# Forgetting-attention heads 0 to 3 projected as three seven-product chunks behind the z units, with two attention workers and the token sums on GpSimd

## The chip, the cores and the metric

The kernel runs on one core of one Trainium2 chip. The metric is the device time of one execution in microseconds (us); the number to beat is the median of three runs. Engine names are those of the profile: PE is TensorE (PEld its weight loads), DVE VectorE, ACT ScalarE, POOL GpSimd, SP SyncE. PE reads its operands from the on-chip memory and writes banks of 128x512 float32, which the other engines empty.

## The reference

One decoder block on 512 tokens of width 1024, all float32: a gated delta rule with 8 heads (called GDN) and a forgetting attention with 8 heads (called FOX) side by side, merged by two sigmoid gates, and a squared-ReLU MLP behind it.

```python
u = rmsnorm(x, norm_mix_g)
gq, gk, gv, gz, ga, gb, fq, fk, fv, ff, gate_a, gate_b = split(u @ w_in)
# A: causal conv(4)+SiLU on gq,gk,gv; L2 norm; exact chunked gated delta rule -> o_a
y_a = (rmsnorm(o_a, gdn_norm_g) * silu(gz)) @ w_proj_gdn
# B: per head RMSNorm of fq, fk; c = cumsum(log_sigmoid(ff + bias)); for each block of 128 queries
s = q @ k.T * d**-0.5 + c[queries, None] - c[None, keys]        # causal
o_b = softmax(s) @ v
y_b = o_b @ w_proj_fox
h = x + (sigmoid(gate_a) * y_a + sigmoid(gate_b) * y_b) @ w_out
out = h + relu(rmsnorm(h) @ w_up)**2 @ w_down
```

## The kernel before

**Number format.** Every large product is made in three passes: weights and activations are each split into a rounded part `hi` and a remainder `lo`, and PE adds hi·hi, hi·lo and lo·hi. The weights of `w_in` come in *units* of 128x1024 (512 KB). `seq` (L151 to L187) lists all units in the order in which they are used. `unit()` (L260) hands out the next one and, while it does, splits units two places ahead (`LA_SPLIT`) with an ACT copy (`hi`, L256) and a DVE subtraction (`lo`, L257), and loads units three places ahead (`LA_RAW`).

**Two ways of projecting.** `dense()` (L269) takes one unit and makes 24 matmuls of 128x512 (L275, L276, L279): the z units (`zgate`, L1071) and the GDN units (`project`, L592, which follows with a convolution of three DVE steps and a SiLU on ACT) go this way. `stream()` (L981) takes *chunks* of 512 output columns and computes each by seven products of quarter size instead of eight (Strassen's scheme in Winograd's form), named P1 to P7. One product is one unit and 24 matmuls of 128x256 (L1011). The weight quarters P1, P2, P3 are plain loads on the SP queue; those of P5, P6, P7, P4 are sums, and are made by an adding DMA on the POOL queue onto a quarter that is on the chip already (`load`, L219). The other operand, the sums of token quarters, is made once by `factors_u` (L426), which reads the normalised tokens back from DRAM (`ud`), subtracts on DVE (L448) and splits (L286, L287), into `uforms`. Each product is added into its quarter of the output by an ACT copy or a DVE addition (L991, L993). A chunk holds at most two of three PE banks at a time (`mmfree`).

**FOX heads 0 to 3 before** use neither: `fox_pair` (L950) makes two heads from six units, with 288 matmuls of 128x256 (L961, L962, L964) and no saved product. Heads 4 to 7 are the first three chunks of `stream`, and the gates four more.

**Work in the background.** The rest runs as generators in `tasks`. `tick()` (L127) advances each of them by one step; `dense`, `zgate`, `fox_pair` and `stream` call it after every few microseconds of projection. The tasks that matter here are:
- `head` (L612): four steps that turn a GDN head's q, k, v into the matrices of the chunked rule; the fourth waits until `decays` (L560) has made that head's decay matrices.
- `group_chain` (L831): once the four heads of a group are done, `invert` (L659) inverts the triangular matrices, with a loop of 31 pairs of DVE instructions (L681, L683) that gives way to the next tick whenever its counted cost passes `INV_STEP[g]`; then `scan` (L781) runs the recurrence over four chunks.
- `decays(1, ...)`: starts its work when group 0's chain is gone.
- `fox_worker` (L866): takes FOX heads from `fq`, one after the other, and runs softmax attention on them in about ten ticks. `hold[0]` keeps workers from taking a new head.
- `outputs_in` (L1111): waits until the stream's last chunk has begun and all chains and workers are done, then reads the GDN outputs back; `merge_gdn` in the stream's last places needs it.

**Order.** The Python order gives the priorities; a planner with its own estimate of durations then places every engine's instructions, so the small matmuls of the tasks lie among the large ones. The main line (L1086 to L1102) is: z units 0 to 4; GDN group 0 (12 units); `fox_pair(0)`; start of `factors_u`; `fox_pair(1)`; z units 5 to 7; GDN group 1 (12 units, with attention held); then the stream of 49 products (`STREAM`), the projections behind both branches, and the MLP, which the change does not touch.

Of the kernel before, what the change touches and what calls it, by code (L numbers as in the profile page):

```python
# [7 lines left out]
F32 = mybir.dt.float32  # L8
# [7 lines left out]
P = 128  # L16
# [23 lines left out]
LA_SPLIT = 2  # L40
INV_STEP = (2500, 900)


def hybrid_block(tc, a, out):
# [106 lines left out]
    seq = [("w_ab", 0)] + [("w_z", i) for i in range(NZ1)]  # L151
    seq += [("w_gdn", i) for i in range(12)] + [("w_fox", i) for i in range(12)]
    seq += [("w_z", i) for i in range(NZ1, H)] + [("w_gdn", 12 + i) for i in range(12)]

# [45 lines left out]
    def load(n):  # L200
        nme, i = seq[n]
        if nme in FACTOR:
            w, c, s_ = i
            q, old = FACTOR[nme]
            if old is None:
                if w == "w_st":
                    raw = (swp if nme == "P1" else wraw).tile([P, D], F32, tag="raw", name=nm("sraw"))
                else:
                    raw = fresh[2 if nme == "P2" else s_].tile([P, D], F32, tag="raw", name=nm("draw"))
                nc.sync.dma_start(raw, a[w][c, q, s_])  # L210
            elif (nme, i) in LONE:
                if n not in begun:
                    begin(n)
                raw = begun[n]
                nc.gpsimd.dma_start(raw, a[w][c, 2, s_], accum_op=ALU.add)
            else:
                raw = factors[old, i]
                assert seq.index((old, i)) < len(units)
                nc.gpsimd.dma_start(raw, a[w][c, q, s_], accum_op=ALU.add)  # L219
            factors[nme, i] = raw  # L220
            raws[n] = raw, [slice(0, D)]
            return
        w = 256 if nme == "w_ab" else D
        raw = wraw.tile([P, D], F32, tag="raw", name=nm("raw"))
        cuts = [slice(0, 512), slice(512, D)] if 0 < n < 3 else [slice(0, w)]
        for c in cuts:
            nc.sync.dma_start(raw[:, c], a[nme][i][:, c])
        raws[n] = raw, cuts
# [6 lines left out]
    def prefetch_new(n):  # L235

        for m in range(pos[0], min(len(seq), n)):
            if fresh and m not in raws and seq[m][0] in FACTOR and FACTOR[seq[m][0]][1] is None and seq[m][1][0] != "w_st":
                load(m)
            if seq[m] in LONE and m not in begun:  # L240
                begin(m)
# [39 lines left out]

    def split(src, scale=None, dst=None):

        hi, lo = dst or (page(F32R, "hi")[:, :], page(F32R, "lo")[:, :])
        if scale is None:
            act.copy(hi, src)  # L286
            vec.tensor_tensor(lo, src, hi.bitcast(F32), op=ALU.subtract)  # L287
        else:
# [137 lines left out]
    def factors_u():  # L426
        lo, hi = slice(0, 256), slice(256, 512)
        for part in range(2):
# [9 lines left out]
            for p in ("P5", "P7", "P6", "P3"):  # L438
                yield
                x = s1 if p == "P5" else s2  # L440
                for f in range(2):
# [5 lines left out]
                                    "P3": (c[k + 4][:, lo], s2[:, o], ALU.add)}[p]  # L447
                    vec.tensor_tensor(x[:, o], in0, in1, op=op)  # L448
                xh_, xl_ = split(x)
                for f in range(2):  # L450
# [387 lines left out]

    def gdn_group(g, box):
        AT = atp.tile([P, NI, P], F32, tag="AT", name=nm("AT"))  # L840
        hd = drp.tile([5, NCH, P, G, P], F32, tag=f"hd{g}", name=f"hd{g}")
        hts = []
        for i in range(G):
            h = g * G + i
            ys = []
            for j in range(3):
                ys.append(project(h, j))
                tick()
            hts.append(start(head(h, AT, *ys, box, hd)))
        return start(group_chain(g, AT, hd, hts))  # L850


    fq = []
    hold = [False]
    taken = [0]
# [10 lines left out]
    def fox_worker(after=None):  # L866
# [3 lines left out]
        while taken[0] < H:  # L870
            if taken[0] >= len(fq) or hold[0]:
                yield
                continue
# [75 lines left out]

    def fox_pair(hp):  # L950
        vts = ([], [])
        for pn in range(3):
            us = [unit("w_fox"), unit("w_fox")]
            pg2 = [page(s="fqk"), page(s="fqk")]
            for t2 in range(2):
                ps = mmps("fx")
                for tb in (2 * t2, 2 * t2 + 1):
                    o = ps[:, (tb % 2) * 256:(tb % 2 + 1) * 256]
                    for k in range(KT):
                        w = us[k // 4][0][:, (k % 4) * 256:(k % 4 + 1) * 256]  # L960
                        mm(o, uhi[k][:, cs(tb)], w, start=(k == 0), stop=False)  # L961
                        mm(o, ulo[k][:, cs(tb)], w, start=False, stop=False)  # L962
                    for k in range(KT):
                        mm(o, uhi[k][:, cs(tb)], us[k // 4][1][:, (k % 4) * 256:(k % 4 + 1) * 256], start=False,  # L964
                           stop=(k == KT - 1))
                    if tb % 2 == 0:
                        tick()
                if pn < 2:
                    act.copy(pg2[t2], ps)
                else:  # L970
                    for j in range(2):
                        (vec.tensor_copy if j else act.copy)(
                            v3(pg2[j][:, 2 * t2 * P:(2 * t2 + 2) * P], 2), v3(ps[:, :], 2)[:, :, cs(j)])
                tick()
            if pn < 2:
                fq.append((2 * hp + pn, pg2, vts[pn]))
            else:
                for v, x in zip(vts, pg2):
                    v += [x[:, cs(c)] for c in range(NCH)]

    def stream(parts, other):  # L981

# [11 lines left out]

        for p, c in STREAM:
            if p is None:
# [16 lines left out]
            done = parts[c][2]  # L1013
            at[0] = c
            if p == "P1":
# [73 lines left out]
    start(decays(0, box, gt))  # L1089
    fws = [start(fox_worker())]  # L1090
    ch0 = gdn_group(0, box)
    fox_pair(0)
    fu = start(factors_u())
    fox_pair(1)
    start(decays(1, box, ch0))
    hold[0] = True
    for h in range(NZ1, H):
        zgate(h)
    ch1 = gdn_group(1, box)
    hold[0] = False  # L1100
    finish(fu)
    fws += [start(fox_worker()) for _ in range(1, NFW)]  # L1102

# [37 lines left out]
    parts += [gate_chunk(i, to) for to in (sga, mg) for i in range(2)]  # L1141
    stream(parts, merge_gdn)

# [296 lines left out]
def _layout(inputs):  # L1440
# [20 lines left out]
    fx = w[:, 4112:7184].reshape(D, 3, H, P)  # L1461
    pan = []
    for hp in range(2):
        for h in (2 * hp, 2 * hp + 1):
            pan.append(np.concatenate([fx[:, 0, h], fx[:, 1, h]], axis=1))
        pan.append(np.concatenate([fx[:, 2, 2 * hp], fx[:, 2, 2 * hp + 1]], axis=1))
    o["w_fox"] = c(np.stack(pan).reshape(6, 2, 4, P, 256).transpose(0, 1, 3, 2, 4).reshape(12, P, D))
    q, k, v = [[fx[:, j, h] for h in range(H)] for j in range(3)]
# [3 lines left out]

    st = np.stack(st).reshape(7, 2, 4, P, 2, 256)
    o["w_st"] = c(np.stack([st[:, j, :, :, l] for j, l in ((0, 0), (0, 1), (1, 1), (1, 0))], 1)
                  .transpose(0, 1, 3, 2, 4).reshape(7, 4, 1, P, D))
    o["w_z"] = units(w[:, 3072:4096])
# [43 lines left out]
```

## Time and profile before

| what | value |
|---|---|
| runs of before | 981.11, 982.70, 982.94 us (median 982.7) |
| span of the profiled execution | 980.2 us, 2.5 us under the median; the page gives no other time for it |
| PE busy | 970.8 us, 99% |
| DVE, ACT, POOL busy | 710.9, 605.0, 240.2 us |
| granted TensorE clock | 1.000 |
| L961, L962, L964 (`fox_pair`) | first at 122.4 us, last at 213.2 us |
| L1011 (`stream`) | first at 324.7 us, last at 543.5 us |

A PE instruction is drawn from its start to its modelled end, and the next one starts before that end. A busy PE therefore says only that something was under way; what a matmul costs is read from the distance between starts, or from the chain of waits, which cuts overlapping instructions at the next start. A stage is judged by its own window, since the mean over the span mixes stages with different loads on DVE and ACT.

### The profile page before, as it was taken

The numbers are of one execution on the slowest core, as the hardware profiler recorded it, in microseconds if no ns is written. First come the engines' busy times: TensorE is split into PE (matmuls) and PEld (weight loads), VectorE is DVE, ScalarE is ACT, GpSimd is POOL, SyncE is SP. The second block draws the span as 40 slices with busy tenths as digits, with TensorE's granted clock in tenths as the row PEclk, the third lists the DMA queues.
The fourth block names the chain that finished last, engine by engine and source line by source line (L and its number), as shares of the span: only waits on it lengthen the run. The fifth ranks groups of instructions, "written<-read, shape, count | busy, mean of one in ns | idle before, by whom it ended". The sixth has DMA issues, their size and how long they took to land.

```text
span 980.2 us, 17198 instructions
## 1 busy us (share of the span) xinstructions
PE 970.8 (99%) x6545; PEld 874.8 (89%) x6545; DVE 710.9 (73%) x1204; ACT 605.0 (62%) x1050; POOL 240.2 (25%) x236
## 2 busy tenths in 40 slices
PE   8999999999999999999999999999999999999998
PEld 6788899998888999999999888889989989988986
DVE  6877778566577789855656535889896697698596
ACT  7766444766564787867656422678755765666761
POOL 1544120202533513522320005312121121121110
PEclk9999999999999999999999999999999999999999
DMA  7647662475437885757887735688798888889884
GB/s 266 213 135 223 174 158 90 130 239 181 129 116 228 189 166 141 197 129 166 236 201 215 273 103 171 125 181 173 190 188 196 187 173 206 181 175 202 186 166 119
DMA packets 93442, 174.38 MB, mean 178 GB/s; under 512 B 8016, under 2 KB 49200, under 8 KB 93360
## 3 DMA queue, kind: packets, MB, share of 16 engines
q1 hardware_dynamic: 78928, 120.85, 38.8%
q0 software_dynamic: 14432, 52.44, 30.5%
q8 instruction: 51, 0.84, 0.4%
q14 instruction: 31, 0.25, 0.1%
HBM read 152.25 MB, written 21.02 MB: 177 GB/s over the span
## 4 chain that ended last, share of the span: by engine, by line
PE 92%; DVE 4%; DMA 2%; ACT 1%; issue 1%; SPq 0%; DVEq 0%
PE mlp L1171 36%; PE st L1011 12%; PE mm L279 8%; PE mm L276 8%; PE mm L275 8%; PE fx L964 2%; PE fx L961 2%; PE fx L962 2%; PE fo L944 2%; PE sc L919 1%; PE pT L935 1%; DVE lo L257 1%; PE kk L639 1%; PE kq L647 1%; DMA ux<-ud 1%; PE v L797 1%
## 5 line engine op out<-in xcount | busy, mean ns | idle before, releaser
L1402 ACT CAST hi<-draw 128x1024 fp32r<-128x1024 f32 x124 | 130.0, 1050 | 118.4 <-PE mlp L1171 100.4
L1409 DVE TENSOR_TENSOR lo<-draw,hi 128x1024 fp32r<-128x1024 f32 x124 | 151.3, 1222 | 44.8 <-ACT hi L1402 41.6
L256 ACT CAST hi<-raw 128x1024 fp32r<-128x1024 f32 (+1 forms) x62 | 62.9, 1021 | 82.6 <-PE mm L276 59.5
L1171 PE MATMUL mlp<-hi,shi 128*128 128x512 f32 x280 | 109.5, 391 | 0.1
L1171 PE MATMUL mlp<-hi,slo 128*128 128x512 f32 x280 | 109.1, 390 | 0.0
L1171 PE MATMUL mlp<-lo,shi 128*128 128x512 f32 x280 | 109.0, 389 | 0.0
L257 DVE TENSOR_TENSOR lo<-raw,hi 128x1024 fp32r<-128x1024 f32 (+1 forms) x62 | 73.9, 1197 | 29.1 <-ACT hi L256 13.4
L1171 PE MATMUL mlp<-shi,lo 128*128 128x256 f32 x448 | 90.3, 283 | 0.0
L1171 PE MATMUL mlp<-slo,hi 128*128 128x256 f32 x448 | 90.3, 283 | 0.0
L1171 PE MATMUL mlp<-shi,hi 128*128 128x256 f32 x448 | 90.3, 283 | 0.0
L276 PE MATMUL mm<-ulo,hi 128*128 128x512 f32 x216 | 85.0, 394 | 1.2 <-DVE ulo L290 1.2
L275 PE MATMUL mm<-uhi,hi 128*128 128x512 f32 x216 | 85.0, 395 | 0.0
L257 DVE TENSOR_TENSOR lo<-sraw,hi 128x1024 fp32r<-128x1024 f32 x49 | 60.7, 1240 | 20.9 <-ACT hi L256 20.1
L1171 PEld LDWEIGHTS mlp<-shi,hi 128*128 128x128 f32 x448 | 70.6, 192 | 0.9
L1171 PEld LDWEIGHTS mlp<-shi,lo 128*128 128x128 f32 x448 | 69.9, 192 | 0.0
L1171 PEld LDWEIGHTS mlp<-slo,hi 128*128 128x128 f32 x448 | 69.8, 192 | 0.0
L256 ACT CAST hi<-sraw 128x1024 fp32r<-128x1024 f32 x49 | 51.3, 1047 | 26.6 <-PE st L1011 16.2
L1171 PEld LDWEIGHTS mlp<-hi,shi 128*128 128x128 f32 x280 | 52.6, 188 | 11.1 <-issue 0.7
L1171 PEld LDWEIGHTS mlp<-lo,shi 128*128 128x128 f32 x280 | 52.6, 188 | 11.1
L1171 PEld LDWEIGHTS mlp<-hi,slo 128*128 128x128 f32 x280 | 52.6, 188 | 10.3
L219 POOL DMA_DIRECT2D draw<-w_d x30 | 26.3, 876 | 129.9 <-DVE lo L1409 120.8
L219 POOL DMA_DIRECT2D draw<-w_u x32 | 27.7, 866 | 122.6 <-DVE lo L1409 120.0
(336 smaller groups left out, 2466.6 us busy)
## 6 DMA issues: line engine op xcount, KB each, us to landing
draw<-w_u POOLq DMA_DIRECT2D x32, 512.0 KB, 5.7
draw<-w_d POOLq DMA_DIRECT2D x32, 512.0 KB, 6.5
sraw<-w_st POOLq DMA_DIRECT2D x28, 512.0 KB, 5.9
draw<-w_d SPq DMA_DIRECT2D x26, 512.0 KB, 4.4
raw<-w_gdn SPq DMA_DIRECT2D x24, 512.0 KB, 3.8
draw<-w_u SPq DMA_DIRECT2D x24, 512.0 KB, 4.4
sraw<-w_st SPq DMA_DIRECT2D x21, 512.0 KB, 5.5
hd<-hd SPq DMA_DIRECT2D x34, 256.0 KB, 5.4
```

The lines of the kernel that those rows point to most:

```text
L219: nc.gpsimd.dma_start(raw, a[w][c, q, s_], accum_op=ALU.add)
L256: act.copy(hi[:, c], raw[:, c])
L257: vec.tensor_tensor(lo[:, c], raw[:, c], hi[:, c].bitcast(F32), op=ALU.subtract)
L275: mm(o, w, rhi(k), start=(k == 0), stop=False)
L276: mm(o, w, rlo(k), start=False, stop=False)
L279: mm(o, lo[:, k * cols:(k + 1) * cols], rhi(k), start=False, stop=(k == KT - 1))
L944: mm(po[:, cs(i)], vt[c], st[i][:, cs(c)], start=(c == 0), stop=(c == i))
L961: mm(o, uhi[k][:, cs(tb)], w, start=(k == 0), stop=False)
L1011: mm(o, u, w, start=first and t == 0 and k == 0 and j == 0 and x is hi, stop=x is lo and k == 3, skip_group_check=True)
L1171: return (lambda *args, **kw: tc.keep_in_program_order(f(*args, **kw))) if self.pinned[0] else f
L1402: pact.copy(hi, raws[m][0])
L1409: pvec.tensor_tensor(lo, raws[m][0], hi[:, :].bitcast(F32), op=ALU.subtract)
```

## The change

- `fox_pair`, its weights `w_fox` and `hold` go. FOX heads 0 to 3 become three chunks of the same `stream` function (weights `w_sf`, laid out like those of the other chunks), in an order `EARLY` that is cut from the start and the end of `STREAM`.
- z units 5 to 7 move ahead of these products, directly behind GDN group 0. The first two GDN units of group 1 are projected inside `EARLY`, where the big stream has its first two `merge_gdn`; `gdn_group` takes them from `ahead`.
- `factors_u` starts after the first head of group 0, and its sums and remainders go to POOL (16 subtractions of 128x256 and 8 of 128x512) instead of DVE.
- Two `fox_worker` run from the start and are never held.
- `INV_STEP[0]` falls from 2500 to 1600: the inversion of group 0 gives way seven times instead of five.
- `decays(1, ...)` is started behind `EARLY`.

```diff
-INV_STEP = (2500, 900)
+INV_STEP = (1600, 900)
...
-    seq += [("w_gdn", i) for i in range(12)] + [("w_fox", i) for i in range(12)]
-    seq += [("w_z", i) for i in range(NZ1, H)] + [("w_gdn", 12 + i) for i in range(12)]
+    seq += [("w_gdn", i) for i in range(12)]
+    EARLY = [("P1", 0), ("P2", 0), ("P5", 0), ("P1", 1), ("P3", 0), ("P6", 0), ("P2", 1), ("P7", 0), ("P5", 1), ("P4", 0),
+             ("P3", 1), ("P6", 1), ("P1", 2), ("P2", 2), ("P7", 1), ("P5", 2), ("P4", 1), ("P3", 2), ("P6", 2), (None, 0),
+             ("P7", 2), (None, 1), ("P4", 2)]
+    seq += [("w_z", i) for i in range(NZ1, H)]
+    seq += [(p, ("w_sf", c, 0)) if p else ("w_gdn", 12 + c) for p, c in EARLY]
+    seq += [("w_gdn", 14 + i) for i in range(10)]
...
-                    vec.tensor_tensor(x[:, o], in0, in1, op=op)
-                xh_, xl_ = split(x)
+                    pool.tensor_tensor(x[:, o], in0, in1, op=op)
+                xh_, xl_ = split(x, lo_by=pool)
...
-                ys.append(project(h, j))
+                ys.append(ahead.pop(0) if ahead else project(h, j))
                 tick()
             hts.append(start(head(h, AT, *ys, box, hd)))
+            if between and i in between:
+                between[i]()
...
-            if taken[0] >= len(fq) or hold[0]:
+            if taken[0] >= len(fq):
...
-    fws = [start(fox_worker())]
-    ch0 = gdn_group(0, box)
-    fox_pair(0)
-    fu = start(factors_u())
-    fox_pair(1)
-    start(decays(1, box, ch0))
-    hold[0] = True
+    fws = [start(fox_worker()) for _ in range(NFW)]
+    fu = []
+    ch0 = gdn_group(0, box, {0: lambda: fu.append(start(factors_u()))})
     for h in range(NZ1, H):
         zgate(h)
-    ch1 = gdn_group(1, box)
-    hold[0] = False
-    finish(fu)
-    fws += [start(fox_worker()) for _ in range(1, NFW)]
+    finish(*fu)
+    v01, v23 = ([], []), ([], [])
+    ahead = []
+    stream([fox_chunk((None, v01), (0, v01[0])), fox_chunk((2, v23[0]), (1, v01[1])), fox_chunk((3, v23[1]), (None, v23))],
+           EARLY, lambda: ahead.append(project(G, len(ahead))), False)
+    start(decays(1, box, ch0))
+    ch1 = gdn_group(1, box, ahead=ahead)
```

More of the change, by code (lines that the diff above doesn't have):

```diff
@@ L205, in load @@
             if old is None:
-                if w == "w_st":
+                if w in ("w_st", "w_sf"):
                     raw = (swp if nme == "P1" else wraw).tile([P, D], F32, tag="raw", name=nm("sraw"))
@@ L237, in prefetch_new @@
         for m in range(pos[0], min(len(seq), n)):
-            if fresh and m not in raws and seq[m][0] in FACTOR and FACTOR[seq[m][0]][1] is None and seq[m][1][0] != "w_st":
+            if fresh and m not in raws and seq[m][0] in FACTOR and FACTOR[seq[m][0]][1] is None and seq[m][1][0] not in ("w_st", "w_sf"):
                 load(m)
@@ L280, in dense, with split @@
         return ps
-    def split(src, scale=None, dst=None):
+    def split(src, scale=None, dst=None, lo_by=None):
         hi, lo = dst or (page(F32R, "hi")[:, :], page(F32R, "lo")[:, :])
@@ L286, in split @@
             act.copy(hi, src)
-            vec.tensor_tensor(lo, src, hi.bitcast(F32), op=ALU.subtract)
+            (lo_by or vec).tensor_tensor(lo, src, hi.bitcast(F32), op=ALU.subtract)
         else:
@@ L837, in group_chain, with gdn_group @@
         yield from scan(g, AT, hd, got)
-    def gdn_group(g, box):
+    def gdn_group(g, box, between=None, ahead=()):
         AT = atp.tile([P, NI, P], F32, tag="AT", name=nm("AT"))
@@ L846, in gdn_group @@
             for j in range(3):
-                ys.append(project(h, j))
+                ys.append(ahead.pop(0) if ahead else project(h, j))
                 tick()
             hts.append(start(head(h, AT, *ys, box, hd)))
+            if between and i in between:
+                between[i]()
         return start(group_chain(g, AT, hd, hts))
     fq = []
-    hold = [False]
     taken = [0]
@@ L948, in fox_worker, with stream @@
             stores.append(start(store_late(obd[h], o)))
[L950 to L981, printed above, removed]
+    def stream(parts, order, other, main):
         bank = {}
@@ L993, in to @@
                     vec.tensor_tensor(x, x, ps, op=op)
-        for p, c in STREAM:
+        for p, c in order:
             if p is None:
@@ L1013, in stream @@
             done = parts[c][2]
-            at[0] = c
+            if main:
+                at[0] = c
             if p == "P1":
@@ L1141, in hybrid_block @@
     parts += [gate_chunk(i, to) for to in (sga, mg) for i in range(2)]
-    stream(parts, merge_gdn)
+    stream(parts, STREAM, merge_gdn, True)
     ot2 = start(outputs_in2())
@@ L1461, in _layout @@
     fx = w[:, 4112:7184].reshape(D, 3, H, P)
[L1462 to L1467, printed above, removed]
     q, k, v = [[fx[:, j, h] for h in range(H)] for j in range(3)]
@@ L1471, in _layout @@
     st += [w[:, n + T * i:n + T * i + T] for n in (7192, 8216) for i in range(2)]
-    st = np.stack(st).reshape(7, 2, 4, P, 2, 256)
-    o["w_st"] = c(np.stack([st[:, j, :, :, l] for j, l in ((0, 0), (0, 1), (1, 1), (1, 0))], 1)
-                  .transpose(0, 1, 3, 2, 4).reshape(7, 4, 1, P, D))
+    sf = [np.concatenate(b, axis=1) for b in
+          ((v[0], v[1], q[0], k[0]), (q[2], k[2], q[1], k[1]), (q[3], k[3], v[2], v[3]))]
+    for name, m in (("w_sf", sf), ("w_st", st)):
+        m = np.stack(m).reshape(len(m), 2, 4, P, 2, 256)
+        o[name] = c(np.stack([m[:, j, :, :, l] for j, l in ((0, 0), (0, 1), (1, 1), (1, 0))], 1)
+                    .transpose(0, 1, 3, 2, 4).reshape(len(m), 4, 1, P, D))
     o["w_z"] = units(w[:, 3072:4096])
```

## The prediction

> **What bounds the kernel now.** I read the page first, its busy times and the chain that ended last; then what PE waited for; then the load of each engine stage by stage.
>
> ```profile
> span 980.2 us, 17198 instructions
> PE 970.8 (99%) x6545; PEld 874.8 (89%) x6545; DVE 710.9 (73%) x1204; ACT 605.0 (62%) x1050; POOL 240.2 (25%) x236
> ...
> PE 92%; DVE 4%; DMA 2%; ACT 1%; issue 1%; SPq 0%; DVEq 0%
> ```
>
> PE carries the span, and 92% of the chain. All the time that PE is not drawn busy is 980.2 - 970.8 = 9.4 us. The waits of PE, longest first in total, say how little of that a better order could win:
>
> ```profile
> PE mm L276 <- DVE ulo L290: 1.2, 2, 0.7
> ...
> PE Q L741 <- ACT AT L725: 0.5, 1, 0.5
> ```
>
> Nine such waits are listed, none over 1.2 us; the first lies in the start-up. The windows cut the mix into group 0, the two FOX pairs, z and the turn to group 1, group 1, and the stream in three parts (each engine: busy us and instructions):
>
> ```profile
> 72.00:122.00 50.00, 50.00 (x264) 42.44 (x263) 38.69 (x76) 27.95 (x76) 14.71 (x12) 1.00 0.69 196
> 122.00:213.00 91.00, 90.52 (x925) 88.55 (x924) 59.78 (x146) 51.70 (x102) 14.35 (x14) 1.00 0.51 151
> 213.00:255.00 42.00, 42.00 (x254) 36.58 (x253) 25.65 (x64) 24.92 (x44) 10.02 (x9) 1.00 0.54 170
> 255.00:325.00 70.00, 70.00 (x356) 58.70 (x355) 50.61 (x91) 39.85 (x92) 29.08 (x25) 1.00 0.56 158
> 325.00:400.00 75.00, 74.83 (x606) 72.15 (x605) 66.02 (x169) 58.32 (x128) 27.73 (x27) 1.00 0.78 174
> 400.00:480.00 80.00, 79.80 (x809) 76.07 (x808) 49.38 (x112) 62.04 (x123) 23.73 (x21) 1.00 0.66 172
> ```
>
> The columns are the stretch, then PE, PEld, DVE, ACT, POOL, the granted clock, DMA share and GB/s. The reader should see PE full in every row, at full clock, and 325 to 400 as the fullest stage for the others: DVE 66.02 of 75 us (88%), with PE short by 0.17. So the kernel is PE-bound, and an edit counts by the PE work that it removes, unless it makes another engine late.
>
> **The PE work removed.** Overlapping matmuls can't be priced by their duration. In the chain, which cuts them at the next start, I read the distance:
>
> ```profile
> 154.28 0.96 PE fx L964 x8
> 494.60 2.88 PE st L1011 x24
> 563.80 1.81 PE mm L279 x8
> ```
>
> A 128x256 matmul is 0.96/8 = 0.120 us in the FOX pairs and 2.88/24 = 0.120 in the stream; a 128x512 one 1.81/8 = 0.226. Counts:
>
> ```profile
> L961 PE MATMUL fx<-hi,uhi 128*128 128x256 f32 x192 | 48.5, 288 | 0.0
> L962 PE MATMUL fx<-hi,ulo 128*128 128x256 f32 x192 | 47.8, 284 | 0.0
> L964 PE MATMUL fx<-lo,uhi 128*128 128x256 f32 x192 | 28.4, 285 | 0.0
> ```
>
> Out: 3 x 192 = 576, 69.1 us. In: 3 chunks x 7 products x 24 = 504, 60.5 us. Difference **-8.6 us**. The z units and two GDN units only move; their matmuls are the same. Small work between the products stays in number, but how it cuts them may change:
>
> ```profile
> 128.91 0.37 PE L961 MATMUL fx<-hi,uhi 128*128 128x256 f32 x1
> 129.11 0.28 PE L962 MATMUL fx<-hi,ulo 128*128 128x256 f32 x1
> ```
>
> The first product matmul behind other work takes 129.11 - 128.91 = 0.20 us to the next start, 0.08 over the usual. Thirty cuts more or fewer would be 2.4 us either way; I take 0 and keep 2.4 for the range.
>
> **What the products ask of the other engines.**
>
> ```profile
> L256 ACT CAST hi<-sraw 128x1024 fp32r<-128x1024 f32 x49 | 51.3, 1047 | 26.6 <-PE st L1011 16.2 <-DMA sraw<-w_st 8.3 <-PE mm L276 1.4
> L257 DVE TENSOR_TENSOR lo<-sraw,hi 128x1024 fp32r<-128x1024 f32 x49 | 60.7, 1240 | 20.9 <-ACT hi L256 20.1 <-DMA hd<-conv 0.7
> L991 ACT COPY fqk<-st 128x512 f32<-128x512 f32 x12 | 7.0, 585 | 0.0
> L993 DVE TENSOR_TENSOR fqk<-fqk,st 128x512 f32<-128x512 f32 x9 | 6.1, 676 | 1.8 <-ACT fqk L991 1.8
> L969 ACT COPY fqk<-fx 128x512 f32<-128x512 f32 x8 | 4.6, 580 | 3.3 <-PE fx L964 3.3
> L972 DVE COPY fqk<-fx 128x256 f32<-128x256 f32 x4 | 1.7, 419 | 1.0 <-ACT fqk L972 1.0
> ```
>
> 21 units instead of 12 need 9 more splits: ACT 9.4 us, DVE 11.2. Emptying the banks costs ACT 7.0 and DVE 6.1 (12 and 9 instructions, as these three-chunk rows) against 4.6 and 1.7 that go, with four more ACT copies. So DVE +15.6, ACT about +11, before the token sums leave DVE:
>
> ```profile
> L448 DVE TENSOR_TENSOR ux<-ux,ux 128x256 f32<-128x256 f32 x12 | 5.3, 481 | 0.1
> L287 DVE TENSOR_TENSOR lo<-ux,hi 128x512 fp32r<-128x512 f32 x8 | 6.3, 792 | 4.8 <-ACT hi L286 4.8
> L573 POOL TENSOR_TENSOR gu<-upper,glo 128x512 fp32r<-128x512 f32 x8 | 9.4, 1177 | 0.0
> ```
>
> With four further sums at the same price (1.9) DVE gives back 13.5; its net is +2.1 us over some 200, covered by the third of DVE that idles from 122 to 325 (59.78 + 25.65 + 50.61 of 203 busy). No row shows such a sum on POOL. Eight remainders at 1.177 are 9.4 us; a sum of half the width lies between half of 1.177 and all of it, 16 of them 9.4 to 18.8. I take the half, since the row is of the same operation: 18.8 us in all, beside 14.71 of 50 in group 0. Nobody needs the sums before the third product, over 20 us behind group 0; without that cover POOL's 18.8 us would delay it whole.
>
> **Queues.** Twelve w_fox loads leave SP; 9 plain loads come to it and 12 adding DMAs to POOL:
>
> ```profile
> raw<-w_fox SPq DMA_DIRECT2D x12, 512.0 KB, 4.7
> sraw<-w_st POOLq DMA_DIRECT2D x28, 512.0 KB, 5.9
> ux<-ud SPq DMA_DIRECT2D x8, 256.0 KB, 5.5
> ```
>
> Issue is behind earlier POOL work, landing 5.9 us. A unit is loaded three ahead, 3 x 2.88 = 8.6 us, which covers 5.9 with 2.8 to spare; the stream lives on the same margin at 325 to 400. The eight ux loads pass ahead of GDN loads on SP: 2.1 MB over 50 us are 42 GB/s on 196, cost nothing while units come three dense units (3 x 24 x 0.226 = 16 us) ahead, and if that failed at most one landing, 5.5 us.
>
> **The tasks.** Ticks between group 0's end and group 1's first new projection were 24 (pairs) + 6 (z), and are 6 + 23. The inversion gives way twice more, so the chain of group 0 ends two ticks later, and `decays(1)` begins about two ticks into group 1 instead of one ahead. Head 4 then waits some four ticks; heads 5 to 7 find their matrices. Group 1's last head still starts with the big stream, so nothing behind it moves: 0. If the delay did pass on, it is 2 x 2.88 = 5.8 us.
>
> The inversion's DVE work:
>
> ```profile
> L683 DVE TENSOR_TENSOR X<-X,tmp 128x126 f32<-128x126 f32 (+22 forms) x62 | 18.8, 303 | 1.5
> L681 DVE TENSOR_TENSOR tmp<-E,X 128x126 f32<-128x126 f32 (+22 forms) x62 | 17.9, 289 | 1.4
> ```
>
> One group is 18.4 us. Before: six pieces of 3.1 us, beside half a split (0.62) per tick: 3.7 us of DVE per 2.88 us of PE, and PE lost 0.48 in 91. After: eight pieces of 2.3 beside a split and 3/7 of an addition (1.24 + 0.29): 3.8. Nearly the same excess, so I take 0. Bounds: 8 x (3.8 - 2.88) = 7.6 us lost if nothing is ready ahead, and 0.9 won if the idle of 122 to 213 and 325 to 480 (0.48 + 0.17 + 0.20) goes. The end of hold moves attention: head 0 enters at the eighth entry of EARLY, head 3 at the last, ten ticks each, so it ends some four projections into group 1, and two heads leave the full stage at 325.
>
> **Sum.** 980.2 - 8.6 = 971.6 us of span; with the 2.5 us between span and median, **974.1 us**; I say 974.
>
> **The rivals.**
>
> *B, products starve while the inversion runs* (half of the 7.6, up to all of it): 974.1 + 3.8 = 977.9, to 981.7. For it: DVE would be near 90% there. Against it: the row 325 to 400, this very mix at 88%, where PE lost 0.17.
>
> *C, the change frees no engine: POOL's sums hold DVE up in group 0.* DVE has 50 - 38.69 = 11.3 us free there. If DVE stood still during all 18.8 us, PE would lose 7.5: 981.6, no change that a measurement of this kernel can tell (0.2%, 2 us). For it: the same short DVE instruction stretches at times:
>
> ```profile
> L683 DVE TENSOR_TENSOR X<-X,tmp x62: 174/264/1465, 144.4 to 399.9; 128x126 f32<-128x126 f32 x6, 128x30 f32<-128x30 f32 x4, 128x56 f32<-128x56 f32 x4, 128x78 f32<-128x78 f32 x4
> ```
>
> Median 0.264, longest 1.465 us; the difference is about the 1.177 of a POOL instruction. Against it: most of group 0's DVE work is convolution, read from a bank. The Trainium skill (SBUF — State Buffer, § Who interferes with whom) has it that a DVE instruction with two inputs on chip memory waits for a GpSimd instruction that reads there, and one with a single such input does not. By that rule only the nine remainders of group 0 are held, each by one POOL instruction, 9 x 1.177 = 10.6 us, under the 11.3 free, and the sum stays; the stretched row agrees with it.
>
> *D, slower: ACT swaps function tables in group 1.* Attention's exp and the projections' SiLU need different tables, and hold kept them apart:
>
> ```profile
> 255.00:325.00 70.00, 0.00 (x0) 1.00 0.56 158
> ```
>
> That is the busy time of exp's line L924 in the window of group 1: none. Where z units met attention, the ACT timeline shows:
>
> ```profile
> 226.54 1.28 ACT L924 ACT_TABLE_LOAD   x1
> 227.84 0.62 ACT L924 ACTIVATE p<-p,fsm 128x384 f32<-128x384 f32 x1
> ...
> 231.68 1.28 ACT L1082 ACT_TABLE_LOAD   x1
> 232.98 0.60 ACT L1082 ACTIVATE proj<-mm 128x512 f32<-128x512 f32 x1
> ```
>
> From the end of EARLY to the fourth projection of group 1 exp and SiLU alternate, some 12 swaps of 1.28 = 15.4 us. If ACT were the last to finish there, all of it is PE's: 974.1 + 15.4 = 989.5; from 9 uncovered swaps (11.5 us, over the 8.6 + 2.0) the kernel is slower. Against it: ACT has 30 us free in 255 to 325, and PE was full from 213 to 255, where exp and SiLU did alternate. The Trainium skill (ScalarE: Activation LUTs, § What ACT_TABLE_LOAD costs) counts a drain of 1.38 us with each load, 2.66 together; 12 would be 32 us and the kernel near 1006. The rows show 1.28 and the next instruction 0.02 later, so I go by them.
>
> **Chances.** Full gain: 0.68, 974, own range 971 to 977 (0.9 and 2.4 below, 2.4 above). B 0.16, C 0.08, D 0.08. Range 970 to 981.7: 974.1 less 0.9, 2.4 and 0.8 (half of what lies between the lowest run and the median, 981.11 and 982.7), up to the ends of B and C; D stays out. Faster by over 0.2% (under 980.7): the first and most of B, 0.83. Within 0.2%: C and B's end, 0.09. Slower: D, 0.08.
>
> **What would show it.** Right: 504 more L1011-type matmuls at 0.120 and none of fx; big stream's first matmul about where it was, with less attention behind it; PE's waits still a few us. B: PE waiting for `lo` of L257 in the early products. C: L257 stretched in group 0 and PE waiting on DVE there. D: over ten table loads in group 1, PE waiting for ACT. Wrong altogether if the pitch of the early products is not 0.120, or the GDN chain of group 1 ends behind the stream.

## The result and the profile after

| | before | after |
|---|---|---|
| median of runs | 982.8 us (981.1 to 982.9) | 1008.1 us (1005.2 to 1012.3) |
| ratio, with 95% interval | | 1.0261 [1.0231, 1.0292] |
| profiled execution, span | 980.2 us | 1003.5 us (time 1005.2 us) |
| granted clock, mean | 1.000 | 0.987 |

The kernel is 2.6% slower, by 25 us; 974 was predicted, 34 us less than was measured. Page of the changed kernel: span, busy times, shares of the chain.

```profile
span 1003.5 us, 17133 instructions
PE 969.1 (97%) x6473; PEld 869.6 (87%) x6473; DVE 719.6 (72%) x1194; ACT 611.0 (61%) x1057; POOL 275.6 (27%) x272
...
PE 81%; DVE 6%; DMA 5%; issue 4%; ACT 2%; POOL 1%; SPq 0%; POOLq 0%; ACTq 0%; DVEq 0%
```

The 72 matmuls are gone (6545 to 6473), yet PE's share of the chain fell from 92% to 81%, and 1003.5 - 969.1 = 34.4 us of the span now have no matmul drawn, against 9.4. Over the whole span no other engine became full. PE's waits (line, releaser: us in total, times, longest; `L987` is the product line of `stream`):

```profile
PE mm L281 <- DVE conv L605: 10.4, 3, 5.8
PE Qp L713 <- DVE Xd L695: 10.2, 1, 10.2
```

Two new entries: the GDN projections of group 0 wait for a bank that the convolution (`conv`, DVE) has to empty, and the small matmuls `Qp` inside the inversion wait for the inversion's DVE loop. The windows of the changed kernel, cut at these places (stretch, busy us of PE, PEld, DVE, ACT, POOL, granted clock, DMA share, GB/s):

```profile
95.00:120.00 25.00, 16.11 (x67) 12.79 (x66) 15.31 (x30) 13.42 (x34) 18.23 (x18) 0.80 0.67 198
...
180.00:210.00 30.00, 18.38 (x278) 17.74 (x277) 19.81 (x47) 15.07 (x21) 8.30 (x8) 0.83 0.54 129
...
250.00:330.00 80.00, 78.47 (x471) 67.57 (x470) 51.54 (x109) 58.13 (x126) 30.57 (x27) 1.00 0.43 129
```

Of 25 us at 95 and of 30 at 180, PE misses 8.9 and 11.6: 20.5 of the 25 us of extra empty time. Over the whole of neither stretch is an engine full: DVE is at 61% and 66%, POOL at 73% and 28%. In the second, though, that mean hides DVE, as will be seen. The clock adds a smaller part: it was 0.80 and 0.83 instead of 1.00, and what that cost while PE worked is some 5 us (worked out under the clock, at the end). Together these two places make about 26 of the 34 us.

How the first stop comes about can be followed across four engines, in the timelines of PE, POOL, ACT and DVE of the changed kernel (start, duration, engine, line, what; in brackets the idle time before it and who ended it):

```profile
88.06 1.98 PE L285 MATMUL mm<-uhi,lo 128*128 128x512 f32 x8
...
91.08 2.26 POOL L594 TENSOR_TENSOR eb<-em,row 128x512 f32<-128x512 f32 x1
93.29 1.44 POOL L454 TENSOR_TENSOR ux<-ux 128x256 f32<-128x256 f32 x2
...
94.76 0.62 ACT L292 CAST hi<-ux 128x512 fp32r<-128x512 f32 x1 [4.07 <-POOL ux L454]
...
96.30 0.70 ACT L602 ACTIVATE conv<-mm,c_conv 128x512 f32<-128x512 f32 x1
...
97.04 2.32 DVE L605 SCALAR_TENSOR_TENSOR conv<-mm,c_conv,conv 128x511 f32<-128x511 f32 x3 [0.27 <-ACT conv L602]
...
99.50 0.47 PE L281 MATMUL mm<-uhi,hi 128*128 128x512 f32 x1 [3.10 <-DVE conv L605]
```

Two sums stand on POOL behind a decay product; ACT stands 4.07 us before the `hi` copy of the sum; the copy that begins to empty a projection's bank comes behind that `hi` on ACT, the three convolution steps behind the copy on DVE, and PE, which wants the bank, has stood for 3.10 us. The bank that the copy begins to empty at 96.30 must be the one that PE had filled by 90.04 (88.06 + 1.98), since the next projection's matmuls end only behind 96.30: it was ready for over six us. Nobody was in a hurry for that sum. ACT ran nothing else in those 4.07 us, and so the wait of a background instruction became PE's wait.

The longer wait in this stage, 5.8 us up to 114.86, is not a wait for a sum. DVE's timeline shows what it stood before:

```profile
107.97 1.13 DVE L647 SCALAR_TENSOR_TENSOR AT<-kk,ssk,eb 128x128 f32<-128x128 f32 x4 [4.04 <-PE kk L645]
```

DVE stood 4.04 us for `kk`, small matmuls of a `head` that PE came to at 106.88, late by its first stop and the slow clock behind it; the convolution steps for the next bank came behind that on DVE. I read the larger wait as a consequence of the smaller one; no run separates the two.

The second stop, in the waits of all engines from 180 to 212 us of the changed kernel, and one row of POOL's timeline:

```profile
...
PE Qp L713 <- DVE Xd L695: 10.2, 1, 10.2
ACT X L704 <- DVE Xd L695: 9.6, 1, 9.6
...
ACT hi L262 <- DMA sraw<-w_sf: 5.2, 1, 5.2
...
DVE lo L263 <- ACT hi L262: 2.8, 1, 2.8
```

```profile
174.74 0.88 POOL L225 DMA_DIRECT2D sraw<-w_sf  x1 [9.20 <-DVE X L689]
```

Read from the bottom: DVE stands 2.8 us before a remainder whose `hi` is late, ACT 5.2 before that `hi` because its adding DMA is late, and that DMA was issued at 174.74, after POOL had waited 9.20 us for DVE. The loop of the inversion stands among these on DVE. It ends late, and then PE (10.2) and ACT (9.6) stop in front of their instructions that use its result, with stream products behind them.

These waits are the smaller part of the lateness. Windows cut at the loop itself, from its first to its last instruction, in the kernel before and in the changed one:

```profile
143.49:170.50 27.01, 27.01 (x228) 27.01 (x228) 22.05 (x73) 10.04 (x16) 1.07 (x2) 1.00 0.34 99
```

```profile
159.16:198.20 39.04, 28.55 (x236) 28.14 (x235) 33.50 (x80) 14.15 (x20) 10.96 (x11) 0.93 0.83 185
```

The loop took 39.0 us instead of 27.0, and DVE's work in it grew by nearly as much, from 22.05 to 33.50 us; its idle time stayed near 5. The weight splits alone went from four (4.89 us) to eleven (13.40). DVE was busy for 86% of the loop, and PE came to `Qp` at 189.14 (199.33 less the wait of 10.19), 30 us after the loop had begun.

### The profile page after: what moved, and what is told of

It is laid out like the page before. It is cut to its first block, busy times and chain, and to the rows that moved or that the text cites. A ratio compares the mean times of both kernels' runs of the same rounds, so it can differ in the third digit from the quotient of the medians.

```text
span 1003.5 us, 17133 instructions
## 1 busy us (share of the span) xinstructions
PE 969.1 (97%) x6473; PEld 869.6 (87%) x6473; DVE 719.6 (72%) x1194; ACT 611.0 (61%) x1057; POOL 275.6 (27%) x272
## 4 chain that ended last, share of the span: by engine, by line
PE 81%; DVE 6%; DMA 5%; issue 4%; ACT 2%; POOL 1%; SPq 0%; POOLq 0%; ACTq 0%; DVEq 0%
PE mlp L1147 30%; PE st L987 14%; PE mm L281 8%; PE mm L282 8%; PE mm L285 7%; DMA sraw<-w_st 2%; PE sc L926 2%; PE fo L951 2%; DMA sraw<-w_sf 2%; DVE lo L263 1%; DMA draw<-w_u 1%; PE pT L942 1%; DVE conv L605 1%; PE o L824 1%; PE v L803 1%
## 5 line engine op out<-in xcount | busy, mean ns | idle before, releaser
L262 ACT CAST hi<-sraw 128x1024 fp32r<-128x1024 f32 x70 | 73.1, 1046 | 67.1 <-PE st L987 24.2
L263 DVE TENSOR_TENSOR lo<-sraw,hi 128x1024 fp32r<-128x1024 f32 x70 | 86.7, 1240 | 29.8 <-ACT hi L262 26.8
L281 PE MATMUL mm<-uhi,hi 128*128 128x512 f32 x216 | 87.9, 409 | 10.4 <-DVE conv L605 10.4
L262 ACT CAST hi<-raw 128x1024 fp32r<-128x1024 f32 (+1 forms) x50 | 50.5, 1015 | 58.5 <-PE mm L282 46.0
L263 DVE TENSOR_TENSOR lo<-raw,hi 128x1024 fp32r<-128x1024 f32 (+1 forms) x50 | 60.9, 1221 | 24.1 <-ACT hi L262 19.9
L1147 PEld LDWEIGHTS mlp<-lo,shi 128*128 128x128 f32 x280 | 52.6, 188 | 11.1
L605 DVE SCALAR_TENSOR_TENSOR conv<-mm,c_conv,conv 128x509 f32<-128x509 f32 (+2 forms) x72 | 52.4, 744 | 13.5 <-ACT conv L602 12.7
```

Of the source, the lines that this page charges most:

```text
L262: act.copy(hi[:, c], raw[:, c])
L263: vec.tensor_tensor(lo[:, c], raw[:, c], hi[:, c].bitcast(F32), op=ALU.subtract)
L281: mm(o, w, rhi(k), start=(k == 0), stop=False)
L605: vec.scalar_tensor_tensor(y[:, s:], ps[:, :T - s], cw[:, i:i + 1], y[:, s:], op0=ALU.mult, op1=ALU.add)
L1147: return (lambda *args, **kw: tc.keep_in_program_order(f(*args, **kw))) if self.pinned[0] else f
```

## The experiments

Each was timed against before on the same chip; ratios carry 95% intervals. The median of before was 982 to 983 us throughout. Where an edit is shown against run 3 or 6, it is what differs from that run.

**1 to 4: the sums' engine and the size of the inversion's pieces.** The sums back on DVE (1), pieces of 2500 (2) and of 900 (3) in the inversion, and 1 with 3 (4):

```diff
-                    pool.tensor_tensor(x[:, o], in0, in1, op=op)
-                xh_, xl_ = split(x, lo_by=pool)
+                    vec.tensor_tensor(x[:, o], in0, in1, op=op)
+                xh_, xl_ = split(x)
...
-INV_STEP = (1600, 900)
+INV_STEP = (2500, 900)      # 2
+INV_STEP = (900, 900)       # 3, 4
```

> The changed kernel with the token sums and their remainders back on DVE, still in group 0. Theory 1: the sums on POOL cost about 12 us, because ACT's rounded copies wait in order for each POOL sum (4.07 us once), the convolution behind them comes late, PE stops for 3.1 and 5.8 us and its clock is halved after each stop. Then this runs in about 996 us and PE no longer waits for the convolution near 100 us. Rival (group 0 would be late anyway, since the sums' ACT and DMA work was moved there): within 3 us of 1008, with the same waits.

> The changed kernel with the inversion of group 0 in its old steps (2500). Theory 2: PE waits 10.2 us because the matmuls behind the inversion stand in PE's order among the first products, before DVE can have finished; fewer steps put them earlier by two products (5.8 us), so the wait grows to about 16 us and the time to about 1014. Rival (the smaller steps are what slows the inversion): the wait shrinks and the time falls to about 1000.

> The changed kernel with the inversion of group 0 in steps of 900, as group 1 has. Theory 2: the matmuls behind the inversion move six ticks back, over 15 us, the 10.2 us wait goes and with it the halved clock; about 996 us. Rival (the early products starve DVE, adding DMAs and ACT whatever the order): the wait is replaced by waits of the products for their splits, and the time stays within 4 us of 1008.

> Both edits: sums on DVE, inversion steps of 900. If theories 1 and 2 name both losses, about 984 us or a little less (24 us back), level with the kernel before. If the early products themselves are starved, 992 or more.

| run | us | ratio |
|---|---|---|
| 1 | 1003.9 | 1.0229 [1.0207, 1.0251] |
| 2 | 1022.9 | 1.0413 [1.0397, 1.0428] |
| 3 | 1000.2 | 1.0175 [1.0151, 1.0199] |
| 4 | 996.2 | 1.0136 [1.0121, 1.0151] |

Waits from 80 to 120 us, first of the changed kernel, then of run 1:

```profile
PE mm L281 <- DVE conv L605: 8.9, 2, 5.8
ACT hi L292 <- POOL ux L454: 7.1, 4, 4.1
```

```profile
PE mm L281 <- DVE conv L605: 8.8, 2, 6.9
...
ACT hi L292 <- DVE ux L454: 7.9, 5, 3.8
```

POOL wasn't the cause of this stop: with the sums on DVE, ACT stands before `hi` for 7.9 us instead of 7.1, and PE loses 8.8 instead of 8.9; what the 4.2 us are was not separated. I had expected 996 if POOL were the cause, and about 1008 if not. The piece size does decide the second stop. PE waits of run 3, whole span:

```profile
PE mm L281 <- DVE conv L605: 10.2, 2, 5.8
PE st L987 <- ACT fqk L967: 3.2, 1, 3.2
PE st L987 <- DVE fqk L969: 2.4, 1, 2.4
```

`Qp` is gone from the list, the convolution wait is as it was, and two new ones come near 370 us, 5.6 together: the time falls by 7.9 us, although the wait of 10.2 is gone. How the smaller pieces do it is seen in the loop's own window and in PE's row of `Qp`, both of run 3:

```profile
160.60:206.25 45.65, 44.71 (x366) 43.67 (x364) 39.51 (x95) 26.46 (x43) 12.50 (x13) 1.00 0.79 176
```

```profile
216.25 0.63 PE L713 MATMUL Qp<-Xd,AT 32*32 32x32 f32 x28
```

The inversion is not faster: its loop takes 45.7 us instead of 39.0, with DVE as full (39.51 us, 87%). But PE comes to `Qp` only 56 us after the loop began, instead of 30, and finds the result. Larger pieces (2) bring a `Qp` wait of 11.0 us, where 16 was expected, more convolution waits (17.9), and a time 9 us over the forecast. Run 4 expected 984 if the two stops were all; 12 of the 24 us came.

**5: the move of the sums alone, in the kernel before.** `factors_u` of before, on DVE, started behind head 0 of group 0.

```diff
-    def gdn_group(g, box):
+    def gdn_group(g, box, between=None):
...
+            if between and i in between:
+                between[i]()
...
-    ch0 = gdn_group(0, box)
+    fu = []
+    ch0 = gdn_group(0, box, {0: lambda: fu.append(start(factors_u()))})
     fox_pair(0)
-    fu = start(factors_u())
...
-    finish(fu)
+    finish(*fu)
```

> The kernel before, with one part of the change alone: the token sums start behind the first head of group 0, on DVE. Theory 1 as the sums on DVE left it (the loss near 100 us comes from the place of the sums, not from their engine: ACT takes its work in order, and scaling and rounding the sums waits there for loads and sums, ahead of the convolution's copy that PE needs): 9 to 13 us slower than before, 992 to 996, with PE waiting for the convolution near 100 us. Rival (the wait near 100 us belongs to the changed order behind group 0, such as the earlier z units): within 2 us of before.

993.6 us, 1.0115 [1.0099, 1.0131]. PE waits:

```profile
PE mm L275 <- DVE conv L599: 7.8, 2, 5.2
```

As expected by the theory that the place counts: 11 us for this edit alone, without an early product, an earlier second worker or a sum on POOL.

**6: the same work, spaced.** Run 3 with the steps of `factors_u` further apart: one more `yield` between the loads and the scaling, and one between each sum and its split.

```diff
             yield
             yield
+            yield
             for k in c:
                 act.activation(c[k], c[k], AF.Copy, scale=mix_g[:, k:k + 1])
...
                     pool.tensor_tensor(x[:, o], in0, in1, op=op)
+                yield
                 xh_, xl_ = split(x, lo_by=pool)
```

> The changed kernel with inversion steps of 900 (1000.2 us) and the sums' steps spread over twice the ticks: one more tick between load and scaling, one between each sum and its rounding. Theory 1 (what stands too early in ACT's order waits there): most of the 12 us near 100 us go, about 989 us. Rival (group 0 has no room for this work at all, DVE, POOL or DMA being full): 997 to 1003, the wait moved or kept.

989.1 us, 1.0068 [1.005, 1.0086], as expected. Each engine runs as many instructions as in run 3, and 11 us came back. PE waits, and the window of group 0:

```profile
PE mm L281 <- DVE conv L607: 4.2, 2, 3.3
PE st L989 <- ACT fqk L969: 2.9, 1, 2.9
```

```profile
72.00:122.00 50.00, 46.73 (x245) 39.34 (x244) 33.74 (x62) 32.64 (x86) 27.57 (x25) 1.00 0.76 224
```

The clock stays at 1.00 through group 0. This is the fastest version found with the change's products, and still 0.7% slower than before. So most of the first stop came from the order of the work in group 0, not from its amount; a wait of 3.3 us for the convolution is left.

**7 and 8: the decay matrices earlier.** Run 3 (7) and run 6 (8) with `decays(1)` started when group 0 is inverted, not when its chain is over.

```diff
+    def decays_1():
+        while not inverted[0]:
+            yield
+        yield from decays(1, box)
+    start(decays_1())
     stream([...], EARLY, ...)
-    start(decays(1, box, ch0))
```

> The changed kernel with inversion steps of 900, and the decay matrices of group 1 started as soon as group 0 is inverted instead of when its scan is over. Theory 3: the 7.5 us lost near 360 us come from POOL, whose decay work for group 1 is late and stands ahead of the big stream's first adding DMAs; then those go, about 993 us. Rival (the big stream starts with two FOX heads fewer behind it and is slow for other reasons): unchanged, 998 to 1002, or slower because the matrices hold pages that the early products need.

> Both edits on top of inversion steps of 900. If the three places (group 0, the inversion, the decays) hold the whole loss, about 981 to 984 us, at least level with before; if they share a cause, such as full engines, 990 or more.

999.7 us, 1.0186 [1.0165, 1.0207], and 990.2, 1.0082 [1.006, 1.0105]: no gain over 3 and 6, where 993 and at most 984 were expected. In run 7 the loss near 360 us shrinks (7.5 to 2.4 by the distances between PE's starts) and about 5 us appear near 280: moved, not won. That late decays cost the 7.5 us is not borne out.

**9 and 16: the workers.** Run 6 with attention held until group 1 is projected (9); the kernel before with two workers from the start, never held (16).

```diff
# 9
+    hold = [True]
...
-            if taken[0] >= len(fq):
+            if taken[0] >= len(fq) or hold[0]:
...
     ch1 = gdn_group(1, box, ahead=ahead)
+    hold[0] = False
```

```diff
# 16, against before
-            if taken[0] >= len(fq) or hold[0]:
+            if taken[0] >= len(fq):
...
-    fws = [start(fox_worker())]
+    fws = [start(fox_worker()) for _ in range(NFW)]
...
-    fws += [start(fox_worker()) for _ in range(1, NFW)]
```

> The spread kernel (989.1 us) with attention held until group 1 is projected, so that no exp stands among the SiLUs of group 1; heads 0 to 3 then run beside the big stream. Rival D of the prediction (the table swaps cost): over 3 us faster, 986 or less. My reading of the changed kernel's trace (PE 78.47 of 80 us busy in group 1, so the swaps are covered): not faster, and 2 to 8 us slower since the big stream gets two heads more.

> The kernel before with one part of the change alone: two attention workers from the start, never held, so that heads 1 to 3 run among the z units and group 1. Rival D (exp and SiLU swapping ACT's tables costs PE time): 5 us or more slower, with over ten table loads between 213 and 325 us. My reading (the swaps are covered): within 3 us of before, 979 to 986.

Run 9: 1056.2 us, 1.0749 [1.0729, 1.0769], far outside what was expected. PE's longest wait in total:

```profile
PE st L990 <- DVE conv L607: 14.9, 2, 11.6
```

With attention kept out of group 1 the kernel loses 67 us more. What holds the rest up then, perhaps the memory of the waiting heads, was not separated, so this run says nothing on rival D. Run 16: 990.9 us, 1.008 [1.0063, 1.0097], with this window:

```profile
255.00:300.00 45.00, 41.21 (x216) 33.54 (x215) 23.78 (x45) 22.95 (x53) 22.48 (x19) 0.92 0.35 105
```

Freeing the workers costs 7.6 us by itself, as much as rival D had asked for (5 us or more), and ACT is at half load where it is lost. The swaps aren't the price: from 213 to 330 us before had nine table loads and this kernel five. PE's longest wait there is 2.8 us for the convolution at 283.94, with the clock at 0.92 over the window; why the convolution came late was not followed.

**10, 12, 15: other places and engines for the spaced sums.** Run 6 with the sums on DVE (10, the edit of run 1), started one head later (12), or with scaling and `hi` on POOL as well, so that ACT has no part in them (15).

```diff
# 12
-    ch0 = gdn_group(0, box, {0: lambda: fu.append(start(factors_u()))})
+    ch0 = gdn_group(0, box, {1: lambda: fu.append(start(factors_u()))})
# 15
...
-                act.activation(c[k], c[k], AF.Copy, scale=mix_g[:, k:k + 1])
+                pool.tensor_tensor(c[k], c[k], mix_g[:, k:k + 1].to_broadcast([P, T]), op=ALU.mult)
...
-                xh_, xl_ = split(x, lo_by=pool)
+                xh_, xl_ = split(x, lo_by=pool, hi_by=pool.tensor_copy)
```

> The spread kernel with the sums on DVE instead of POOL. With the sums not spread this was worth 4.2 us (steps 1600) and 4.0 us (steps 900). If POOL's price is a lock-out of DVE, it is there whatever the order: 985 us. If it was the waiting for POOL in ACT's order, the spreading has paid for it already, and DVE in group 0 gets too full: 988 to 992.

> The spread kernel with the sums started one head later. Theory 1 says that room in group 0 is what counts: the 5 us still lost between 100 and 140 us shrink, 985 to 987. Rival: the sums then come late for the third early product and PE waits there: 991 or more.

> The spread kernel (989.1 us) with the scaling and the rounded copies of the sums on POOL too, so that ACT has no part in them. Theory 1 (ACT's in-order queue is what hurts group 0): the 5.5 us still lost between 100 and 140 us go, 983 to 986. Rival (POOL, which also serves the heads' root and decay steps, becomes the late one: some 37 us of work for it in group 0): 992 or more, or PE waiting for the sums in the early products.

Run 10: 994.2 us, 1.0129 [1.0112, 1.0147]. Run 12: 1002.4, 1.0212 [1.0195, 1.0229]. Run 15: 995.0, 1.0127 [1.0105, 1.015]. The first is 2 us over the forecast, the other two came out as their rivals had it. The longest PE waits of 12 and of 15, and from 95 to 125 us of 15 a wait of DVE:

```profile
PE st L989 <- ACT fqk L969: 10.0, 4, 7.6
```

```profile
PE mm L281 <- DVE conv L607: 6.7, 1, 6.7
```

```profile
DVE ssk L627 <- POOL ssk L352: 4.7, 2, 3.5
```

Later sums (12) clear group 0 and run into the early products. With ACT out of it (15) the stop is there again: now DVE stands before a step of `head` for POOL, which has the scaling and the copies to do as well. As these waits read, no one engine holds the loss; it goes to whichever queue holds the sums' chain ahead of the bank's emptying. Once spaced, POOL is the better place than DVE, by 5 us.

**11 and 14: the inversion's place.** Run 6 with pieces of 1200 (11); the changed kernel with four more ticks between the end of the inversion's DVE part and `Qp` (14).

```diff
# 14
         yield
+        for _ in range(4 if rest == INV_STEP[0] else 0):
+            yield
         qs = page(s="Q")
```

> The spread kernel with inversion steps of 1200 (nine turns instead of thirteen; 1600 has seven). Theory 2 and the later chain pull apart here: if four ticks earlier still leave DVE ready in time, the later work (decays, big stream, near 350 us) gains and the time is 984 to 987. If PE's order again runs ahead of the inversion, the wait near 190 us is back with some 5 us: 992 to 995.

> The changed kernel, inversion steps of 1600 as they are, but four ticks between the end of the inversion on DVE and the matmuls that need it. Theory 2 (the place of those matmuls in PE's order, not the size of DVE's steps): the 10.2 us wait near 190 us goes as with steps of 900, 996 to 1001. Rival (finer steps let DVE serve the products sooner, the place is nothing): 1005 or more with the wait in its place.

Run 11: 1008.5 us, 1.0262 [1.0236, 1.0288]; run 14: 1018.4, 1.036 [1.0342, 1.0378]. In 11 a `Qp` wait of 6.3 us is back, new ones come near 330 us, and the time is beyond both forecasts: pieces of 900 are not one of many good sizes. In 14 I had expected the stop to go with `Qp`. Waits from 170 to 240 us of run 14:

```profile
PE st L989 <- ACT fqk L969: 11.4, 1, 11.4
ACT X L704 <- DVE Xd L695: 10.6, 1, 10.6
```

`Qp` moved and PE stops all the same, now in front of a product whose bank ACT hasn't emptied, because ACT stands 10.6 us before the copies of the inverse. That `Qp` alone stood too early in PE's order is refuted: the edit left ACT's copies of the inverse where they were, and they stand too early as well. In run 3 these come later too (at 207.50, after a wait of 0.8 us). The inversion is late for PE and for ACT alike.

**13: the removed matmuls alone.** The kernel before with 72 of the 576 FOX matmuls left out.

```diff
-                    for k in range(KT):
+                    for k in range(3, KT):
                         mm(o, uhi[k][:, cs(tb)], us[k // 4][1][:, ...], start=False, stop=(k == KT - 1))
```

> The kernel before with 72 of the 576 FOX matmuls of 128x256 left out (three of eight in the last pass of each token block), so 504 as after the change, everything else as before. If the prediction's first term holds (PE-bound stage, 0.120 us each), 8.6 us faster: 973 to 975. If DVE, ACT or DMA set that stage, less than 5 us of it arrive: 978 or more.

978.9 us, 0.9959 [0.9944, 0.9974]: 4.4 us, not 8.6. A new wait of PE, and the window right behind it:

```profile
PE Tp L720 <- ACT Q L710: 2.4, 1, 2.4
```

```profile
176.86:180.27 3.41, 3.41 (x78) 2.63 (x68) 1.76 (x5) 3.41 (x8) 0.00 (x0) 0.50 0.47 162
```

The wait of 2.4 us and 3.41 us of work at half clock, 1.7 us lost, hold most of what is missing. Take matmuls out of that stage and its chain of small dependent steps, the inversion, is what PE meets next.

## Why the prediction was wrong, point by point

The matmuls were saved as forecast; the prediction failed where it set every stall at 0. Two steps hold most of it: the moved sums and the inversion.

- **"Difference -8.6 us."** Count and pitch held: 72 matmuls fewer, and the early products go at 0.119 us (14 in 1.67 in the chain of the changed kernel):

```profile
217.23 1.67 PE st L987 x14
```

  But "an edit counts by the PE work that it removes" was too much to say of this stage: run 13 got 4.4 of 8.6, with no stream product in it.
- **"Cost nothing while units come three dense units ahead", and the sums covered "over 20 us behind group 0".** This is the larger failing step. The cover was right: the sums were in time for the products. It priced when the result is needed, and not what stands behind each step of the chain load, scale, sum, `hi`, `lo` on ACT, DVE and POOL. Measured: 11 us for the move (run 5), and 11 us back from spacing (run 6 against 3). The only bound set here, 5.5 us, was for a late load; the chain's own waiting had none.
- **"I take the half": 18.8 us on POOL.** By the POOL rows above two sums take 1.44 us, so 16 take 11.5, and with eight remainders at 1.28 it is 21.7 us: a little more. Rival C, which charged this to DVE's standing still beside POOL, had the place right; but run 1 takes the sums off POOL, 4.2 us come back, and the stop stays. Whether C's mechanism is part of the 4.2 was not tested.
- **"Nearly the same excess, so I take 0", bound 7.6.** The second failing step, and rival B's place. B was right that DVE would be near 90% there: it was at 86% over the loop, with eleven splits where eight were counted. B was wrong in what PE would wait for: not the `lo` of a product but the inverse itself, at `Qp`. The sum priced DVE's excess tick by tick and left out where PE and ACT meet the result: PE came to it 30 us after the loop's start, and DVE needed 39. The wait was 10.2 us, over B's bound, with half clock behind it; the pieces of 900 give back 7.9 in all (run 3), and by moving the meeting place, not by a lighter DVE. Against B I had set the row 325 to 400, "this very mix at 88%, where PE lost 0.17". It shows one order of that mix in which nothing is late, and proves nothing for another order.
- **"Landing 5.9 us", with 2.8 to spare.** In the changed kernel the 512 KB adding DMAs of the early products start late, and land in a median of 6.4 us, some slower; from its chain:

```profile
157.42 9.33 DMA sraw<-w_sf
...
174.74 7.20 DMA sraw<-w_sf
```

  Three ahead covers 8.6 us. The first of these is over that, before its late issue is counted.
- **"If the delay did pass on, it is 5.8 us", taken at 0.** Runs 3 and 7 lose 5 to 7 us near 360 or 280 us, where group 1's chain, attention and the big stream's start meet. Bringing the decays forward moves the loss. Its cause is not settled.
- **Rival D, table swaps, 15.4 us.** Not borne out: PE has 78.47 of 80 us from 250 to 330 at full clock, where ACT loads nine tables, and run 16 has fewer loads than before and is slower. Freeing the workers does have a price in the kernel before (7.6 us), by another way.
- **Not in the sum at all: what a stop costs afterwards.** See the clock, below.

Laid end to end: after 1008.1; smaller pieces -7.9; spaced sums -11.1; so 989.1, 6.3 us over before, where a free saving would stand at 974. By the distances between PE's starts, less what before loses in the same stretch, these last 15 us lie in three pieces of about 5 us each, between 100 and 140, 180 and 260, and 340 and 400 us of run 6. The 4 us that run 13 doesn't get either and the price of the freed workers (run 16) may be in them; that is not shown. Their causes stay open, and no version here beats the kernel before.

## What to carry to other kernels

Price background work that is moved by its place in each in-order queue: for every step ask what stands behind it on its engine while it waits for its input, whether or not its result is urgent; the busy share of a stage can hide it (DVE had 66% of one and 86% of the loop in it), and a full neighbouring stage only shows that its own order works. Where a loop grows by the work that is put between its steps, compare its end with the place at which the other engines need it. Before counting a PE saving in full, look in that stage for the longest chain of small dependent steps, and take out the same matmuls alone to see what arrives. Where such a chain holds others up, first try spacing its steps: here two added `yield` lines gave back 11 us, and moving the unspaced sums to another engine 4. Time each setting, since the nearest ones (a start one head later, inversion pieces of 1200) were slower again.

## What the runs showed of the hardware

**A stop of PE can be paid for twice.** The three stretches of half clock at the two places of the changed kernel, and PE's starts behind the stop of 3.10 us:

```profile
100.95:104.36 3.41, 3.41 (x10) 2.63 (x9) 2.55 (x4) 0.00 (x0) 3.41 (x4) 0.50 0.66 218
111.19:118.02 6.83, 3.16 (x8) 2.52 (x9) 5.21 (x10) 4.36 (x7) 3.50 (x5) 0.50 0.86 226
193.11:203.35 10.24, 4.02 (x74) 3.96 (x75) 6.92 (x23) 3.95 (x7) 0.52 (x1) 0.50 0.54 183
```

```profile
100.95 0.61 PE L281 MATMUL mm<-uhi,hi 128*128 128x512 f32 x1
...
104.34 0.41 PE L281 MATMUL mm<-uhi,hi 128*128 128x512 f32 x1
```

PE waited 3.10 us, resumed at 99.50, and from 100.95 to 104.34 the granted clock was halved: eight matmuls at 0.42 instead of 0.23 us, 1.6 us more. In the three stretches PE was busy for 3.41 + 3.16 + 4.02 = 10.6 us, so I estimate the price of the half clock at 5.3 us.

The Trainium skill (TensorE: Matmul & The Clock Gate, § What's actually happening) gives half clock after an idle window of some 3.4 us and full clock after one busy window as long. The 3.41 us of half clock, and multiples of it, agree with that. The idle time does not: the stop here was 3.1 us, in run 13 one of 2.4 was enough, and in run 6 one of 3.3 left the clock at 1.00. What decided here seems to be how the stop lies to a fixed grid of 3.41 us, laid back from the starts of half clock: 1.96 us of the 3.10 fell into the window that ended at 100.95, all of run 13's 2.4 into one window, while run 6's 3.3 was cut into 1.55 and 1.72. That is a reading of the traces, not an experiment.

**Short DVE instructions stretch beside POOL.** Products of 128x4 on DVE in group 0 of the changed kernel, and two instructions of POOL:

```profile
101.38 1.23 DVE L625 TENSOR_TENSOR ssk<-ssk 128x4 f32<-128x4 f32 x1 [0.90 <-POOL ssk L352]
102.54 0.15 DVE L627 TENSOR_TENSOR ssk<-ssk 128x4 f32<-128x4 f32 x1
102.65 1.21 DVE L626 TENSOR_TENSOR ssk<-ssk,kds 128x4 f32<-128x4 f32 x1
...
101.32 1.27 POOL L293 TENSOR_TENSOR lo<-ux,hi 128x512 fp32r<-128x512 f32 x1
102.55 1.28 POOL L594 TENSOR_TENSOR eb<-em,row 128x512 f32<-128x512 f32 x1
```

0.15 us or eight times that; POOL's instructions start just ahead of the two long ones. It agrees with the rule that the prediction weighed, except that the prediction counted only the nine remainders as held, and these small products were held too. It didn't decide the first stop, which stays with the sums on DVE (run 1).
